# Large products of a two-layer hybrid trunk: one unsplit float32 matmul per weight tile instead of three on two-part operands

## The chip, the core and the metric

The kernel runs on one core of one Trainium2 chip. The metric is the device time of one execution in microseconds. The engines are named as the profile names them: PE (TensorE matmul), PEld (TensorE weight load), DVE (VectorE), ACT (ScalarE), POOL (GpSimd) and SP (SyncE, which here issues most transfers).

## The reference

Two layers run over 640 tokens of width 1024: 128 tokens of a prompt and 512 of a sample. Everything is float32.

```
for l in range(2):
    m  = silu(cond) @ w_mod + b_mod                       # nine vectors of 1024
    x  = rmsnorm(h) * (1 + sc1) + sh1
    h += 0.5 * g1 * (silu(x @ wg) * (x @ wu)) @ wd         # 1024 -> 2816 -> 1024
    x  = rmsnorm(h) * (1 + sc2) + sh2
    p  = x @ w_in                                         # 1024 -> 1536
    merged = [ssm(p), window_attention(p), full_attention(p), fourier(p)]
    h += g2 * merged @ w_out                              # 1024 -> 1024
    x  = rmsnorm(h) * (1 + sc3) + sh3
    h += 0.5 * g3 * (silu(x @ wg2) * (x @ wu2)) @ wd2
y = rmsnorm(h)
```

The four heads' inner products (attention, state space, Fourier) are small beside the products with `wg`, `wu`, `wd`, `w_in` and `w_out`; only these last five, called the large products here, are changed.

## The kernel before

The residual lies transposed in on-chip memory, channels on the partitions, in two halves of the tokens (`HALVES`): 256 and 384 columns. A large product takes a weight tile of 128x128 as the stationary operand and a block of 256 or 384 token columns as the moving one, and accumulates in PSUM over the blocks of 128 input channels (8 for 1024 channels). The projection `w_in` has it the other way for two of its three parts: 128 tokens are stationary, and 512 (or 256) weight columns move (`proj_tile`).

No large product is taken in float32 directly. Each operand is split into a high part, rounded to the type float32r, and a low part, the rest, also float32r. `mm3` (lines 258 to 265) then issues three matmuls for each weight tile: high by high, high by low, low by high. `ffn` has the same three written out for its first two feature blocks (lines 666 to 668), where four accumulations go on side by side because the inputs come ready block by block (`LEAD` = 2), and `proj_tile` has them at lines 1013 to 1015.

The split costs work on the other engines:

- Weights: `prep_to` (line 193) copies a piece of a loaded slab to `whi` on ACT (line 209) and subtracts on DVE to get `wlo` (line 210), in a ring of six pairs of buffers. Slabs of 1 MB at most come from HBM through SP into three buffers (`raw`), ahead by what `limit` and `load_limit` allow.
- Inputs: `x_prep` (line 539) makes `xh` on ACT and `xl` on DVE or POOL.
- The feature activations: after silu(gate) times up on DVE (`hx`, line 679) come `hh` on ACT (line 680) and `hl` on DVE (line 681).
- The merged heads: `split` makes a high part on ACT and a low one on DVE.

The order of instructions is that in which the Python code emits them, as the tile framework's scheduler then places them. Side work is emitted by `tick`: every large product reports how many nanoseconds its matmuls should take, and the norms, the stream of `w_mod` (on DVE, from POOL's queue) and the tables of the state space part are emitted when their due time in these nanoseconds has run out. `mm3` reports three times 0.417 ns a column plus 2.5 ns. Due times are `T_SUM` (2300, sum of squares), `T_BC` (5000, broadcast of the norm and `x_prep`), `T_OUT` (6500, output), and the spans `M_P0`, `M_P1` and `M_P2` over which `w_mod` is spread. At the end of each residual phase (`res_phase`) the last `FIN` output blocks run for one half of the tokens, then for the other, so that the first half's norm is made beside the second half's matmuls.

Other matmuls of the kernel are plain float32 already. Those of the Fourier part (`fnet`) are spoken of later. Each of its steps holds these calls, with float32 tiles on both sides, first those of the upper loop, at the end those of the lower one (shortened):

```python
for cs in range(2):
    for cb in range(2):
        nc.tensor.matmul(ps[:, 0:66], u[:, 0, c], dc[:, cs, :], start=True, stop=True)          # L1265
        for kb in range(4):
            nc.tensor.matmul(ps[:, 66:FC], u[:, 1 + kb, c], dl[:, cs, kb, :], ...)              # L1267
        yield
for nb in range(2):
    for half, (c0, w) in enumerate(HALVES):
        for mb in range(2):
            nc.tensor.matmul(ps[:, 0:w], fw[:, mb, ...], f[:, mb, c0:c0 + w], ...)              # L1293
```

Of the kernel before, what the change touches and what calls it, by code (L numbers as in the profile page):

```python
# [17 lines left out]
P = 128  # L18
# [19 lines left out]
FIN = 5  # L38
MARK = (-1, -1)
MARK_P = 5  # L40
# [4 lines left out]
M_P1 = 300  # L45
M_P2 = 340
X_PAT = ("dbdbdbdb", "dbbdbbdb")
# [61 lines left out]

class Net:  # L110
    def __init__(self, tc, a, depth=DEPTH, dump=None):
# [9 lines left out]
        self.ready = {}  # L121
        self.i_use = 0
        self.i_prep = 0
# [7 lines left out]
        self.limit = 0  # L131
        self.load_limit = 0
        self.seg = []
# [9 lines left out]
        self.ahead = 2  # L143
        self.fine = False
        self.marks = ()
# [29 lines left out]
    def load_upto(self, n):  # L175
        while self.i_load < min(n, len(self.slabs), self.load_limit):
            s = self.i_load
            srcs, shape = self.slabs[s]
            t = self.rawp.tile([P, RAW], F32, tag="raw", name="raw")
# [12 lines left out]

    def prep_to(self, n):
        while self.i_prep < min(n, len(self.wq), self.limit):
            sid, f = self.wq[self.i_prep]
            self.load_upto(sid + 1)
            v = f(self.raw[sid])
            k, w = v.shape[1], v.shape[2]
            sl = self.i_ring % self.ring_n
            self.i_ring += 1  # L200
            pool = self.ring_a if sl < RING_A else self.ring_b
            hi = pool.tile([P, 1024], F32R, tag=f"h{sl}", name="whi")
            lo = pool.tile([P, 1024], F32R, tag=f"l{sl}", name="wlo")
            hv = hi[:, 0:k * w].rearrange("p (k n) -> p k n", k=k)
            lv = lo[:, 0:k * w].rearrange("p (k n) -> p k n", k=k)
            with ExitStack() as es:
                for i in self.marks:
                    es.enter_context(self.tc.issue_after(i.ins))
                self.nc.scalar.activation(hv, v, AF.Copy)  # L209
                self.nc.vector.tensor_tensor(lv, v, hv, op=OP.subtract)  # L210
            self.ready[self.i_prep] = (hv, lv)
            self.slab_left[sid] -= 1
            if self.slab_left[sid] == 0:
                self.raw.pop(sid)
            self.load_upto(sid + self.raw_bufs)
            self.i_prep += 1

    def w(self, ahead=2):
        """Next operand of the stream; keeps `ahead` more in preparation."""
        i = self.i_use  # L220
        self.i_use += 1
        self.prep_to(i + 1 + ahead)
        return self.ready.pop(i)

# [43 lines left out]
    def setup(self):  # L268
# [5 lines left out]
        self.raw_bufs = 3  # L274
# [30 lines left out]
    def setup_vectors(self):  # L305
        """small vectors: rows of 128, transposed to columns."""
# [121 lines left out]
    def mod_to(self, n, ns=None):  # L428
        """slabs up to n: spread over the coming ns, or what is left of them now."""
# [46 lines left out]
    def load_x(self):  # L476
# [3 lines left out]
        xin = [self.xp.tile([P, w // P, D], F32, name=f"xin{i}", tag=f"xh{i}") for i, (_, w) in enumerate(HALVES)]  # L480
        junk = self.xp.tile([P, 2, D], F32, name="sqj", tag="xl0")
# [21 lines left out]
    def rstd_from(self, ss, c0, n):  # L503
        """ss [P, n] sums of squares per token -> rs_tok columns."""
# [6 lines left out]
    def norm_bc(self, half):  # L511
        """broadcast of rstd over the partitions, in PSUM [P, width]."""
# [13 lines left out]
    def x_tiles(self, half):  # L526
        w = HALVES[half][1]
        return (self.xp.tile([P, DB, w], F32R, name=f"xh{half}", tag=f"xh{half}"),
                self.xp.tile([P, DB, w], F32R, name=f"xl{half}", tag=f"xl{half}"))

    def x_norm(self, half, rb, k, x):
        """h * rstd of one block."""
        self.nc.vector.tensor_tensor(x, self.hT[half][:, k, :], rb[:, 0:HALVES[half][1]], op=OP.mult)

    def x_prep(self, half, l, j, rb=None, xn=None):
        """x = h rstd A + B as two parts; xn: h rstd, where it is there already."""
        nc = self.nc
        w = HALVES[half][1]
        self.x[half] = xh, xl = self.x_tiles(half)
# [3 lines left out]
        for k in range(DB):  # L543
            kind = X_PAT[half][k]
            t = self.t(w, "xt")
            for s, e, v in parts:
                Ak, Bk = A[:, k, v:v + 1], B[:, k, v:v + 1]
                if rb is None:
                    i_v = nc.vector.tensor_scalar(t[:, s:e], xn[:, k, s:e], Ak, Bk, op0=OP.mult, op1=OP.add)
                else:  # L550
                    i_v = nc.vector.scalar_tensor_tensor(t[:, s:e], self.hT[half][:, k, s:e], Ak, rb[:, s:e],  # L551
                                                         op0=OP.mult, op1=OP.mult)
                    if kind == "d":
                        i_a = nc.scalar.activation(xh[:, k, s:e], t[:, s:e], AF.Identity, bias=Bk)
                        nc.vector.scalar_tensor_tensor(xl[:, k, s:e], t[:, s:e], Bk, xh[:, k, s:e],
                                                       op0=OP.add, op1=OP.subtract)
                    else:
                        nc.scalar.activation(t[:, s:e], t[:, s:e], AF.Identity, bias=Bk)
            if rb is None or kind != "d":
                i_a = nc.scalar.activation(xh[:, k, :], t[:, 0:w], AF.Copy)  # L560
                nc.gpsimd.tensor_tensor(xl[:, k, :], t[:, 0:w], xh[:, k, :], op=OP.subtract)
            if k == (MARK[half] if rb is not None else MARK_P if half == 0 else -1):
                self.marks = (i_v, i_a)
# [33 lines left out]
    def finish_half(self, half, l, j):  # L597
        """norm of a finished half of the residual, spread over the coming matmuls."""
# [33 lines left out]
    def ffn(self, l, j, nxt, chunks, e_pro=None):  # L632
        """j: 0 or 2; nxt: (layer, norm) the next phase reads, or None.
        e_pro: the pool of the tables that are made beside the first N_TAB chunks."""
# [3 lines left out]
        for ci, (c0, n) in enumerate(chunks):  # L638
# [6 lines left out]
            hh = [hp.tile([P, nf, w], F32R, name=f"hh{i}", tag=f"hh{i}") for i, (_, w) in enumerate(HALVES)]  # L645
            hl = [hp.tile([P, nf, w], F32R, name=f"hl{i}", tag=f"hl{i}") for i, (_, w) in enumerate(HALVES)]

            def gate_up(fs, half, wts):
                w = HALVES[half][1]
                xh, xl = self.x[half]  # L650
# [10 lines left out]
                if len(fs) > 1:  # L661
                    for k in range(DB):
                        for i, f in enumerate(fs):
                            for s in range(2):
                                o, (wh, wl) = outs[2 * i + s], wts[f][s]
                                nc.tensor.matmul(o, wh[:, k, :], xh[:, k, :], start=(k == 0), stop=False)  # L666
                                nc.tensor.matmul(o, wl[:, k, :], xh[:, k, :], start=False, stop=False)
                                nc.tensor.matmul(o, wh[:, k, :], xl[:, k, :], start=False, stop=(k == DB - 1))  # L668
                        self.tick(len(fs) * 6 * (w * 0.417 + 2.5))
                else:  # L670
                    for s in range(2):
                        wh, wl = wts[fs[0]][s]
                        self.mm3(outs[s], [(wh[:, k, :], wl[:, k, :], xh[:, k, :], xl[:, k, :]) for k in range(DB)])
                for i, f in enumerate(fs):
# [10 lines left out]
            while f < n:  # L685
                grp = [f + i for i in range(lead if f == 0 else 1)]
                wts = {}
                for ff in grp:
                    wts[ff] = [self.w(self.ahead if len(grp) == 1 else 0) for _ in range(2)]
# [1135 lines left out]
```

## Time and profile before

| | |
|---|---|
| median of 3 runs | 2588.22 us (2588.08 to 2589.85) |
| span of the profiled execution | 2589.3 us |
| PE busy | 2517.7 us, 97% |
| DVE busy | 1507.6 us, 58% |
| ACT busy | 823.6 us, 32% |
| bytes read from HBM | 256.29 MB |

The profile is of one execution. A busy time is the union of an engine's instructions; matmuls overlap one another, so the mean duration of one is longer than the step from one to the next. The time that a matmul holds the engine is therefore read from the starts of neighbours in the timeline. A line number is that of the kernel before; L261 to L263 are the three matmuls of `mm3`, so that every large product through `mm3` shows under these lines.

### The profile page before, as it was taken

To read this page: it belongs to the slowest core of one execution; us is meant where nothing else is said; L and a number is where in the kernel's file an instruction comes from. 1 tells how busy PE (TensorE), PEld (TensorE's weight loads), DVE (VectorE), ACT (ScalarE), POOL (GpSimd) and SP (SyncE) were. 2 spreads that over 40 slices of the span, in tenths; PEclk is the share of its full clock that TensorE was granted. 3 is DMA by queue.
4 is the path that set the end of the run, shared out by engine and by line. 5 is a ranking of instruction groups with operands and counts; after the bars stand their busy time and mean duration, and the time that the engine had idled before them with its cause. 6 is when DMAs were issued, how large, how long until landed. Compare 5 with 4: busy or idle time off the path is not lost.

```text
span 2589.3 us, 41527 instructions
## 1 busy us (share of the span) xinstructions
PE 2517.7 (97%) x17054; PEld 2366.8 (91%) x17054; DVE 1507.6 (58%) x3012; ACT 823.6 (32%) x1547; POOL 387.2 (15%) x782
## 2 busy tenths in 40 slices
PE   5999999999899999999999999999999999999998
PEld 3899999998669899999999999999976799999998
DVE  6888677363667876454456666644546773333333
ACT  3332222242443532222233222223425553222222
POOL 2321111014801211000011001000183010000000
PEclk7999999999999999999999999999999999999999
DMA  7565444231114254333314445432401133222311
GB/s 254 158 182 183 145 147 147 90 101 55 34 35 147 58 168 126 119 111 114 114 50 143 137 125 151 139 106 66 126 18 54 34 98 98 69 82 62 98 49 41
DMA packets 199092, 273.93 MB, mean 106 GB/s; under 512 B 17208, under 2 KB 168472, under 8 KB 198392
## 3 DMA queue, kind: packets, MB, share of 16 engines
q1 hardware_dynamic: 176888, 193.30, 23.7%
q0 software_dynamic: 22016, 78.00, 10.2%
q8 instruction: 134, 2.20, 0.4%
q14 instruction: 54, 0.44, 0.1%
HBM read 256.29 MB, written 14.97 MB: 105 GB/s over the span
## 4 chain that ended last, share of the span: by engine, by line
PE 77%; issue 9%; POOL 7%; DVE 5%; DMA 2%; ACT 1%; SPq 0%; DVEq 0%; POOLq 0%; ACTq 0%
PE gu L261 14%; PE gu L263 14%; PE gu L262 14%; PE y L261 8%; PE y L262 8%; PE y L263 8%; POOL sc L1124 2%; POOL ee L1127 2%; POOL ee L1126 1%; DMA wm<-in_w_mod_dram 1%; POOL sc L1125 1%; DVE wlo L210 1%; DVE xt L551 1%; PE gu L668 1%; PE gu L666 1%
## 5 line engine op out<-in xcount | busy, mean ns | idle before, releaser
L261 PE MATMUL gu<-xh,whi 128*128 128x256 f32 (+1 forms) x2560 | 794.2, 310 | 0.9 <-DVE hx L679 0.9
L263 PE MATMUL gu<-xh,wlo 128*128 128x384 f32 (+1 forms) x2560 | 789.4, 309 | 0.6 <-DVE wlo L210 0.6
L262 PE MATMUL gu<-xl,whi 128*128 128x384 f32 (+1 forms) x2560 | 788.7, 308 | 0.0
L209 ACT ACTIVATE whi<-raw 128x1024 fp32r<-128x1024 f32 (+2 forms) x344 | 328.5, 960 | 875.4 <-PE gu L262 424.8
L210 DVE TENSOR_TENSOR wlo<-raw,whi 128x1024 fp32r<-128x1024 f32 (+2 forms) x344 | 380.2, 1107 | 343.3 <-ACT whi L209 342.9
L261 PEld LDWEIGHTS gu<-xh,whi 128*128 128x128 f32 x2560 | 481.3, 188 | 13.5 <-issue 11.0
L262 PEld LDWEIGHTS gu<-xl,whi 128*128 128x128 f32 x2560 | 482.6, 189 | 1.3 <-issue 1.2
L263 PEld LDWEIGHTS gu<-xh,wlo 128*128 128x128 f32 x2560 | 481.5, 188 | 1.6 <-DVE wlo L210 0.8
L261 PE MATMUL y<-hh,whi 128*128 128x384 f32 (+1 forms) x1408 | 436.0, 311 | 0.5 <-ACT est L957 0.3
L263 PE MATMUL y<-hh,wlo 128*128 128x384 f32 (+1 forms) x1408 | 434.8, 309 | 0.0
L262 PE MATMUL y<-hl,whi 128*128 128x384 f32 (+1 forms) x1408 | 434.6, 309 | 0.0
L389 DVE SCALAR_TENSOR_TENSOR mvec<-wm,cs,mvec 128x512 f32<-128x512 f32 x448 | 319.2, 750 | 20.9 <-DMA wm<-in_w_mod_dram 20.5
L595 DVE SCALAR_TENSOR_TENSOR hT<-y,G,hT 128x128 f32<-128x128 f32 (+1 forms) x432 | 175.8, 436 | 228.5 <-PE y L263 228.2
L261 PEld LDWEIGHTS y<-hh,whi 128*128 128x128 f32 x1408 | 266.1, 190 | 4.7 <-issue 3.7
L262 PEld LDWEIGHTS y<-hl,whi 128*128 128x128 f32 x1408 | 267.1, 190 | 0.5 <-issue 0.4
L263 PEld LDWEIGHTS y<-hh,wlo 128*128 128x128 f32 x1408 | 266.9, 190 | 0.0
L353 POOL DMA_DIRECT2D wm<-in_w_mod_dram x128 | 92.5, 723 | 956.7 <-DVE mvec L389 813.2
L679 DVE TENSOR_TENSOR hx<-sg,gu 128x256 f32<-128x256 f32 (+1 forms) x176 | 85.1, 483 | 119.5 <-ACT sg L677 119.2
L680 ACT ACTIVATE hh<-hx 128x256 fp32r<-128x256 f32 (+1 forms) x176 | 82.9, 471 | 184.6 <-DVE hx L679 184.5
L508 POOL TENSOR_TENSOR rst<-ms,mhalf 128x2 f32<-128x2 f32 (+1 forms) x12 | 11.2, 932 | 854.9 <-DVE ms L507 854.9
L677 ACT ACTIVATE sg<-gu 128x256 f32<-128x256 f32 (+1 forms) x176 | 75.3, 428 | 175.4 <-PE gu L263 170.8
L681 DVE TENSOR_TENSOR hl<-hx,hh 128x256 fp32r<-128x256 f32 (+1 forms) x176 | 86.3, 492 | 51.7 <-ACT hh L680 51.4
(313 smaller groups left out, 3239.8 us busy)
## 6 DMA issues: line engine op xcount, KB each, us to landing
wm<-in_w_mod_dram POOLq DMA_DIRECT2D x128, 512.0 KB, 4.2
raw<-in_ffn_w_gate_dram SPq DMA_DIRECT2D x44, 1024.0 KB, 5.4
raw<-in_ffn_w_up_dram SPq DMA_DIRECT2D x44, 1024.0 KB, 5.5
raw<-in_ffn_w_down_dram SPq DMA_DIRECT2D x24, 1024.0 KB, 5.2
raw<-in_ffn_w_down_dram SPq DMA_DIRECT2D x16, 768.0 KB, 4.9
raw<-in_w_in_dram SPq DMA_DIRECT2D x12, 1024.0 KB, 5.1
wm<-in_w_mod_dram SPq DMA_DIRECT2D x16, 512.0 KB, 5.5
raw<-in_ffn_w_down_dram SPq DMA_DIRECT2D x16, 512.0 KB, 4.1
```

What stands on the lines that cost most here:

```text
L209: self.nc.scalar.activation(hv, v, AF.Copy)
L210: self.nc.vector.tensor_tensor(lv, v, hv, op=OP.subtract)
L261: self.nc.tensor.matmul(out, wh, xh, start=(i == 0), stop=False)
L262: self.nc.tensor.matmul(out, wh, xl, start=False, stop=False)
L263: self.nc.tensor.matmul(out, wl, xh, start=False, stop=(i == n - 1))
L353: self.nc.gpsimd.dma_start(out=t.rearrange("p (j c) -> p j c", j=2), in_=w[kk * 256:(kk + 1) * 256, c0:c0 + 512].rearrange("(j p) c -> p j ...
L389: nc.vector.scalar_tensor_tensor(self.mvec[:, v], w, c, self.mvec[:, v], op0=OP.mult, op1=OP.add)
L595: nc.vector.scalar_tensor_tensor(h, y[:, s:e], G[:, k, v:v + 1], h, op0=OP.mult, op1=OP.add)
L677: nc.scalar.activation(sg[:, 0:w], g, AF.Silu)
L679: nc.vector.tensor_tensor(hx[:, 0:w], sg[:, 0:w], u, op=OP.mult)
L680: nc.scalar.activation(hh[half][:, f, :], hx[:, 0:w], AF.Copy)
L681: nc.vector.tensor_tensor(hl[half][:, f, :], hx[:, 0:w], hh[half][:, f, :], op=OP.subtract)
```

## The change

Every large product is one matmul on float32 operands. `mm3` becomes `mm`, the three matmuls in `ffn` and `proj_tile` become one, and `w()` hands out a view of the loaded slab. `prep_to`, the ring of split weights and the limits go; slabs come into four buffers of their own (`RAW_W`), and a slab is released by `used()` after the products that read it. `x_prep`, the activations and the merged heads write one float32 tile. The times reported to `tick` are those of `mm_ns`, and the spans of `w_mod`, `FIN` and the first chunks of the feature dimension (`CHUNKS4`) get other numbers.

```diff
-RING = 6
-RING_A = 2
+RAW_W = 4
-CHUNKS4 = ((0, 4), (4, 4), (8, 6), (14, 8))
+CHUNKS4 = CHUNKS
-FIN = 5
+FIN = 4
-M_P1 = 300
-M_P2 = 340
+M_P1 = 190
+M_P2 = 215
+def mm_ns(cols):
+    return cols * 0.835 + 3
...
-    def prep_to(self, n):
-        while self.i_prep < min(n, len(self.wq), self.limit):
...
-                self.nc.scalar.activation(hv, v, AF.Copy)
-                self.nc.vector.tensor_tensor(lv, v, hv, op=OP.subtract)
...
+    def w(self):
+        sid, f = self.wq[self.i_use]
+        self.i_use += 1
+        self.load_upto(sid + 1)
+        self.pend.append(sid)
+        return f(self.raw[sid])
+    def used(self):
+        for sid in self.pend:
             self.slab_left[sid] -= 1
             if self.slab_left[sid] == 0:
                 self.raw.pop(sid)
+        self.pend = []
+        self.load_upto((min(self.raw) if self.raw else self.i_load) + RAW_W)
...
-    def mm3(self, out, pairs):
+    def mm(self, out, pairs):
         n = len(pairs)
-        for i, (wh, wl, xh, xl) in enumerate(pairs):
-            self.nc.tensor.matmul(out, wh, xh, start=(i == 0), stop=False)
-            self.nc.tensor.matmul(out, wh, xl, start=False, stop=False)
-            self.nc.tensor.matmul(out, wl, xh, start=False, stop=(i == n - 1))
+        for i, (w, x) in enumerate(pairs):
+            self.nc.tensor.matmul(out, w, x, start=(i == 0), stop=(i == n - 1))
             if self.fine or i == n - 1:
-                self.tick((1 if self.fine else n) * 3 * (out.shape[-1] * 0.417 + 2.5))
+                self.tick((1 if self.fine else n) * mm_ns(out.shape[-1]))
...
+                    nc.vector.scalar_tensor_tensor(t[:, s:e], self.hT[half][:, k, s:e], Ak, rb[:, s:e],
+                                                   op0=OP.mult, op1=OP.mult)
+                    nc.scalar.activation(x[:, k, s:e], t[:, s:e], AF.Identity, bias=Bk)
...
-                    hx = self.t(w, "hx")
-                    nc.vector.tensor_tensor(hx[:, 0:w], sg[:, 0:w], u, op=OP.mult)
-                    nc.scalar.activation(hh[half][:, f, :], hx[:, 0:w], AF.Copy)
-                    nc.vector.tensor_tensor(hl[half][:, f, :], hx[:, 0:w], hh[half][:, f, :], op=OP.subtract)
+                    nc.vector.tensor_tensor(hx[half][:, f, :], sg[:, 0:w], u, op=OP.mult)
...
         for k in range(DB):
-            nc.tensor.matmul(ps[:, 0:n], h, wh, start=(k == 0), stop=False)
-            nc.tensor.matmul(ps[:, 0:n], h, wl, start=False, stop=False)
-            nc.tensor.matmul(ps[:, 0:n], lo, wh, start=False, stop=(k == DB - 1))
+            nc.tensor.matmul(ps[:, 0:n], x[:, k, c0:c0 + P], ws[k // kper][:, k % kper, :], start=(k == 0),
+                             stop=(k == DB - 1))
             if k % 4 == 3:
-                self.tick(12 * (n * 0.417 + 2.5))
+                self.tick(4 * mm_ns(n))
```

## Rows read from the trace of the kernel before

**Rows 1.** The page: span, and busy time, share and records of each engine

```profile
span 2589.3 us, 41527 instructions
PE 2517.7 (97%) x17054; PEld 2366.8 (91%) x17054; DVE 1507.6 (58%) x3012; ACT 823.6 (32%) x1547; POOL 387.2 (15%) x782
```

**Rows 2.** The page: the chain that ended last, by engine

```profile
PE 77%; issue 9%; POOL 7%; DVE 5%; DMA 2%; ACT 1%; SPq 0%; DVEq 0%; POOLq 0%; ACTq 0%
```

**Rows 3.** Stretches: length, busy us (records) of five engines, PE clock, DMA

```profile
54.00:100.00 46.00, 39.97 (x238) 36.63 (x239) 41.38 (x60) 17.93 (x35) 22.48 (x23) 0.88 0.32 102
558.00:852.00 294.00, 279.95 (x1753) 229.79 (x1752) 185.96 (x442) 118.47 (x269) 99.03 (x271) 0.97 0.25 76
852.00:900.00 48.00, 43.92 (x284) 41.04 (x283) 41.77 (x145) 23.45 (x52) 12.46 (x11) 0.93 0.09 21
1819.00:2109.00 290.00, 279.07 (x1779) 230.26 (x1778) 177.88 (x426) 121.15 (x273) 92.67 (x265) 0.98 0.22 68
```

**Rows 4.** Groups by line and shape: records | busy us, mean ns | idle before

```profile
L261 PE MATMUL gu<-xh,whi 128*128 128x256 f32 x1280 | 360.1, 281 | 0.0
L261 PE MATMUL y<-hh,whi 128*128 128x256 f32 x704 | 200.4, 285 | 0.3 <-ACT est L957 0.3
L261 PE MATMUL y<-xh,whi 128*128 128x256 f32 x128 | 36.2, 283 | 0.0
L666 PE MATMUL gu<-xh,whi 128*128 128x256 f32 x128 | 36.0, 292 | 2.3 <-ACT xh L560 2.3
L261 PE MATMUL pu<-xh,whi 128*128 128x256 f32 x32 | 9.1, 284 | 0.0
L1013 PE MATMUL pj<-whi,xh 128*128 128x512 f32 x160 | 63.8, 399 | 0.0
L1013 PE MATMUL pj<-whi,xh 128*128 128x256 f32 x80 | 23.0, 287 | 0.0
L1267 PE MATMUL f<-dl,P 128*128 128x258 f32 x64 | 15.7, 388 | 0.0
```

**Rows 5.** Timeline, PE, split products: start us, us, record

```profile
299.82 0.28 PE L261 MATMUL gu<-xh,whi 128*128 128x256 f32 x1
...
301.11 0.28 PE L263 MATMUL gu<-xh,wlo 128*128 128x256 f32 x1
...
306.90 0.34 PE L261 MATMUL gu<-xh,whi 128*128 128x384 f32 x1
...
310.37 0.34 PE L263 MATMUL gu<-xh,wlo 128*128 128x384 f32 x1
```

**Rows 6.** Timeline, PE, float32 matmuls of the Fourier part (x8: eight records merged)

```profile
650.55 0.33 PE L1265 MATMUL f<-fs,P 128*128 128x66 f32 x2
650.72 1.96 PE L1267 MATMUL f<-dl,P 128*128 128x258 f32 x8
652.52 0.60 PE L1373 MATMUL qkT<-ident,qr 128*128 128x128 f32 x4
...
1936.59 4.58 PE L1293 MATMUL f<-ff,fs 128*128 128x256 f32 x16 [0.69 <-ACT qs L1375]
...
1937.78 0.38 PE L1293 MATMUL f<-ff,fs 128*128 128x256 f32 x1
...
1938.85 0.38 PE L1293 MATMUL f<-ff,fs 128*128 128x256 f32 x1
1939.07 0.49 PE L1293 MATMUL f<-ff,fs 128*128 128x384 f32 x1
...
1940.68 0.49 PE L1293 MATMUL f<-ff,fs 128*128 128x384 f32 x1
```

**Rows 7.** The page: the low part of the weights' split on DVE

```profile
L210 DVE TENSOR_TENSOR wlo<-raw,whi 128x1024 fp32r<-128x1024 f32 (+2 forms) x344 | 380.2, 1107 | 343.3 <-ACT whi L209 342.9
```

**Rows 8.** Timeline around 850 us: broadcast of a norm, first input block after it

```profile
848.20 0.70 PE L521 MATMUL rb<-diag,ones 128*128 128x256 f32 x2 [0.91 <-DVE diag L518]
...
850.11 0.69 ACT L554 ACTIVATE xh<-xt,modT 128x128 fp32r<-128x128 f32 x2 [0.72 <-DVE xt L551]
```

More of the change, by code (lines that the diff above doesn't have):

```diff
@@ L175, in load_upto @@
     def load_upto(self, n):
-        while self.i_load < min(n, len(self.slabs), self.load_limit):
+        while self.i_load < min(n, len(self.slabs)):
             s = self.i_load
             srcs, shape = self.slabs[s]
-            t = self.rawp.tile([P, RAW], F32, tag="raw", name="raw")
+            t = self.wp.tile([P, 2048], F32, tag="raw", name="raw")
             n_el = 1
@@ L214, in prep_to @@
                 self.raw.pop(sid)
[L215 to L223, printed above, removed]
+        self.pend = []
+        self.load_upto((min(self.raw) if self.raw else self.i_load) + RAW_W)
     def later(self, ns, f):
@@ L479, in load_x @@
         ss = self.per.tile([P, 5], F32, name="ss_in", tag="ss", bufs=2)
-        xin = [self.xp.tile([P, w // P, D], F32, name=f"xin{i}", tag=f"xh{i}") for i, (_, w) in enumerate(HALVES)]
-        junk = self.xp.tile([P, 2, D], F32, name="sqj", tag="xl0")
+        xin = [self.xp.tile([P, w // P, D], F32, name=f"xin{i}", tag=f"x{i}") for i, (_, w) in enumerate(HALVES)]
+        junk = self.rawp.tile([P, RAW], F32, name="sqj", tag="raw")[:, 0:2 * D].rearrange("p (a b) -> p a b", a=2)
         xt = [xin[0][:, i] for i in range(2)] + [xin[1][:, i] for i in range(3)]
@@ L524, in norm_bc, with x_tile @@
         return rs
[L526 to L529, printed above, removed]
+    def x_tile(self, half):
+        return self.xp.tile([P, DB, HALVES[half][1]], F32, name=f"x{half}", tag=f"x{half}")
     def x_norm(self, half, rb, k, x):
@@ L538, in x_prep @@
         w = HALVES[half][1]
-        self.x[half] = xh, xl = self.x_tiles(half)
+        self.x[half] = x = self.x_tile(half) if xn is None else xn
         A = self.A[l, j]
@@ L543, in x_prep @@
         for k in range(DB):
-            kind = X_PAT[half][k]
-            t = self.t(w, "xt")
+            t = None if rb is None else self.t(w, "xt")
             for s, e, v in parts:
@@ L548, in x_prep @@
                 if rb is None:
-                    i_v = nc.vector.tensor_scalar(t[:, s:e], xn[:, k, s:e], Ak, Bk, op0=OP.mult, op1=OP.add)
+                    nc.vector.tensor_scalar(x[:, k, s:e], xn[:, k, s:e], Ak, Bk, op0=OP.mult, op1=OP.add)
                 else:
[L551 to L563, printed above, removed]
+                    nc.vector.scalar_tensor_tensor(t[:, s:e], self.hT[half][:, k, s:e], Ak, rb[:, s:e],
+                                                   op0=OP.mult, op1=OP.mult)
+                    nc.scalar.activation(x[:, k, s:e], t[:, s:e], AF.Identity, bias=Bk)
     def sq_start(self):
@@ L644, in ffn @@
                 nf = max(n for _, n in chunks[N_TAB:])
-            hh = [hp.tile([P, nf, w], F32R, name=f"hh{i}", tag=f"hh{i}") for i, (_, w) in enumerate(HALVES)]
-            hl = [hp.tile([P, nf, w], F32R, name=f"hl{i}", tag=f"hl{i}") for i, (_, w) in enumerate(HALVES)]
+            hx = [hp.tile([P, nf, w], F32, name=f"hx{i}", tag=f"hx{i}") for i, (_, w) in enumerate(HALVES)]
             def gate_up(fs, half, wts):
                 w = HALVES[half][1]
-                xh, xl = self.x[half]
+                x = self.x[half]
                 outs = []
@@ L664, in gate_up @@
                             for s in range(2):
[L665 to L669, printed above, removed]
+                                nc.tensor.matmul(outs[2 * i + s], wts[f][s][:, k, :], x[:, k, :], start=(k == 0),
+                                                 stop=(k == DB - 1))
+                        self.tick(len(fs) * 2 * mm_ns(w))
                 else:
                     for s in range(2):
-                        wh, wl = wts[fs[0]][s]
-                        self.mm3(outs[s], [(wh[:, k, :], wl[:, k, :], xh[:, k, :], xl[:, k, :]) for k in range(DB)])
+                        wt = wts[fs[0]][s]
+                        self.mm(outs[s], [(wt[:, k, :], x[:, k, :]) for k in range(DB)])
                 for i, f in enumerate(fs):
@@ L688, in ffn @@
                 for ff in grp:
-                    wts[ff] = [self.w(self.ahead if len(grp) == 1 else 0) for _ in range(2)]
+                    wts[ff] = [self.w() for _ in range(2)]
                 for half in range(2):
                     gate_up(grp, half, wts)
-                    if half == 0 and len(grp) > 1:
-                        self.prep_to(self.i_use + self.ahead)
+                self.used()
                 f += len(grp)
             last = ci == len(chunks) - 1
-            self.res_phase(n, [(hh[i], hl[i]) for i in range(2)], [(f, f) for f in range(n)], (l, j), nxt if last else None)
+            self.res_phase(hx, [(f, f) for f in range(n)], (l, j), nxt if last else None)
         hps.close()
@@ L1023, in proj_u @@
         uT = self.pp.tile([P, 2, 8, NCK], F32, name="uT", tag="ee")
-        wu = [self.w(0) for _ in range(2)]
-        self.prep_to(self.i_use + 2)
-        wf = None
+        wu = [self.w() for _ in range(2)]
+        wf = [self.w()]
         for half, (c0, w) in enumerate(HALVES):
@@ L1029, in proj_u @@
                 self.flush()
-            xh, xl = self.x[half]
+            x = self.x[half]
             for m in range(2):
                 ps = self.b([P, 512], name="pu")
-                self.mm3(ps[:, 0:w], [(wu[m][0][:, k, :], wu[m][1][:, k, :], xh[:, k, :], xl[:, k, :])
-                                      for k in range(DB)])
+                self.mm(ps[:, 0:w], [(wu[m][:, k, :], x[:, k, :]) for k in range(DB)])
                 self.evac(uT[:, m, :, c0 // 8:(c0 + w) // 8].rearrange("p j k -> p k j"),
                           ps[:, 0:w].rearrange("p (k j) -> p k j", j=8))
-            if wf is None:
-                wf = [self.w(0) for _ in range(2)]
-                self.prep_to(self.i_use + 2)
             if half == 1:
@@ L1222, in merged_tiles @@
     def merged_tiles(self):
-        self.mg = [self.x_tiles(h) for h in range(2)]
+        self.mg = [self.x_tile(h) for h in range(2)]
     def split(self, src, blk, c0, w, bias=None):
@@ L1231, in split @@
                 continue
[L1232 to L1233 removed]
+            o = self.mg[half][:, blk, s - h0:e - h0]
             v = src[:, s - c0:e - c0]
             if bias is None:
[L1236 to L1240 removed]
+                nc.scalar.activation(o, v, AF.Copy)
+            else:
+                nc.scalar.activation(o, v, AF.Identity, bias=bias)
     def fnet_load(self, l):
@@ L1544, in out1, with res_phase @@
                 y = self.b([P, 512], name="y1")
-                xh, xl = self.mg[half]
-                self.mm3(y[:, 0:w], [(wd[0][:, i, :], wd[1][:, i, :], xh[:, f, :], xl[:, f, :])
-                                     for i, f in enumerate(OUT1)])
+                x = self.mg[half]
+                self.mm(y[:, 0:w], [(wd[:, i, :], x[:, f, :]) for i, f in enumerate(OUT1)])
                 self.residual(half, db, y, self.G[l, 1])
+                if half == 1:
+                    self.used()
                 yield
-    def res_phase(self, n, xs, order, G, nxt, lead=1):
+    def res_phase(self, xs, order, G, nxt, lead=1):
         def one(db, half, wd):
@@ L1555, in one @@
             y = self.b([P, 512], name="y")
-            xh, xl = xs[half]
-            self.mm3(y[:, 0:w], [(wd[0][:, f, :], wd[1][:, f, :], xh[:, g, :], xl[:, g, :]) for f, g in order])
+            self.mm(y[:, 0:w], [(wd[:, f, :], xs[half][:, g, :]) for f, g in order])
             self.residual(half, db, y, self.G[G])
@@ L1567, in res_phase @@
             k = lead if db == 0 else 1
-            wds = [self.w(self.ahead) for _ in range(k)]
+            wds = [self.w() for _ in range(k)]
             for half in range(2):
@@ L1571, in res_phase @@
                     one(db + i, half, wds[i])
+            self.used()
             db += k
@@ L1574, in res_phase @@
             return
-        wds = [self.w(0) for _ in range(FIN)]
+        wds = [self.w() for _ in range(FIN)]
         h0, h1 = (1, 0) if nxt[1] is None else (0, 1)
@@ L1578, in res_phase @@
             one(DB - FIN + db, h0, wds[db])
-            self.prep_to(self.i_use + min(db, RING - FIN))
         self.x = [None, None]
@@ L1585, in res_phase @@
         self.fine = False
+        self.used()
         self.finish_half(h1, nxt[0], nxt[1])
@@ L1607, in mixer @@
         cva, cka = self.cache_v("cache_axial_kv", l, "cv1"), self.cache_k("cache_axial_kv", l, "ck1")
-        ws = [self.w(0) for _ in range(4)]
+        ws = [self.w() for _ in range(2)]
         for ti in range(5):
             self.proj(1, ti, ws)
-            self.prep_to(self.i_use + min(ti, 2))
             if ti == 0:
@@ L1621, in mixer @@
         self.qr = [qrt[:, 0], qrt[:, 1]]
-        ws = [self.w(0) for _ in range(4)]
+        ws = [self.w() for _ in range(2)]
         self.Pt.append(pp.tile([P, 5, 512], F32, name="P2", tag="P2"))
@@ L1741, in build @@
             n.proj_specs(l)
-            n.seg.append((len(n.wq), len(n.slabs)))
             n.out_specs(l)
             n.ffn_specs(l, "ffn2", CHUNKS4 if l + 1 < depth else CHUNKS)
-        n.seg.append((1 << 30, 1 << 30))
-        n.limit, n.load_limit = n.seg[0]
-        n.open_ring_a()
         e_pro, pro = n.open_pool("pro", side="right")
@@ L1751, in build @@
         n.load_x()
-        e_xs, xs = n.open_pool("xs", side="right")
-        xn = [xs.tile([P, DB, w], F32, name=f"xn{h}") for h, (_, w) in enumerate(HALVES)]
-        n.load_limit = 2
-        n.prep_to(2)
+        xn = [n.x_tile(h) for h in range(2)]
+        n.load_upto(2)
         for i in range(16):
@@ L1765, in build @@
         n.flush()
-        n.load_limit = n.seg[0][1]
+        n.load_upto(RAW_W)
         for h in range(2):
             n.x_prep(h, 0, 0, None, xn[h])
-        e_xs.close()
         n.job_ns = JOB_D
         n.e_mod.close()
-        n.open_ring_b()
         for l in range(depth):
@@ L1793, in build @@
         n.flush()
-        n.close_ring()
     n.es.close()
```

67 lines of the change are left out of this document (12 added, 55 removed).

## The prediction

> **What bounds the kernel now.** I read the busy shares first, then the chain, then the stretches in which PE is not full, and last the single steps of PE. PE is busy for 2517.7 of 2589.3 us, so 71.6 us are idle; no other engine but the weight loads beside it reaches 60% [rows 1]. The chain of work that ended last gives PE 77%, and POOL, the largest other engine, 7% [rows 2]. So the time is close to the sum of what PE is given. Its idle time lies in few places: 6.0 us in the start (54 to 100), 14.1 and 10.9 us in the two mixers, 4.1 us after the first mixer, and in these stretches the granted clock falls to between 0.88 and 0.98 of full speed [rows 3]. The other 36.5 us of idle time I leave as they are. What the reader is to see: a change in DVE or ACT work is worth little here, and a change in what one product costs on PE is worth nearly all of it.
>
> **How many products there are.** A row of one of the three lines counts the triples. Over 256 columns: 1280 + 128 (gate and up), 704 (down), 128 (output projection) and 32 (first projection) make 2272 triples [rows 4]; each weight tile also meets the other half of the tokens, so there are 2272 over 384 columns too. The rest of the projection has 160 triples over 512 and 80 over 256 columns [rows 4].
>
> **What a triple costs.** A matmul's mean duration, 281 ns over 256 columns [rows 4], is no price, since records overlap; the step from start to start is. From 299.82 to 301.11 us lie eleven steps over 256 columns: 117.3 ns each. From 306.90 to 310.37 us lie twenty over 384: 173.5 ns [rows 5]. That is 0.458 and 0.452 ns a column; for 512 columns I take 0.455, so 233 ns. A triple takes 352, 520.5 and 699 ns.
>
> **What one float32 call costs.** This is the term that decides. The kernel already has float32 calls with 128 rows and 128 columns of weights, fresh weights for each, in the Fourier part. In one step of its first loop the code makes one call at L1265 and four at L1267. The timeline has two records at L1265 and eight at L1267, and the next instruction starts 1.80 us after the first of the eight [rows 6]. Over the run L1267 has 64 records where the loops (2 by 2 by 4, two layers) make 32 calls; the split line L1013, which the loops call 160 times over 512 columns, has 160 [rows 4]. So a float32 call leaves two records and a float32r call one. The two do not run side by side: at L1293 eight calls leave 16 records, and six over 256 columns start from 1937.78 to 1938.85, 214 ns a step, six over 384 from 1939.07 to 1940.68, 322 ns a step [rows 6]. That is 0.836 and 0.839 ns a column for a record; I take 0.84, and 1.68 for a call: 430, 645 and 860 ns over 256, 384 and 512 columns. A far upper end is the 1.80 us for eight records of 258 columns, 0.872 ns a column, which has the switch from the product before in it. The step has the loading of the next weights beside it in these rows as it would have in the large products, so nothing is added for that.
>
> **A rule of the Trainium skill.** The page "FP8 and Floating Point Precision", section "TensorE Precision Notes", says that true FP32 takes four passes through the array. At one column per clock at 2.4 GHz that gives an estimate of 427 ns over 256 columns; by it the sum below would be some 20 us smaller, and the reading of one record as the whole call (215 ns) would be wrong. By that rule the trace agrees, with 430 ns for the two records of a call.
>
> **The change part by part.**
>
> Products. A pair (256 and 384 columns) goes from 352 + 520.5 = 872.5 to 430 + 645 = 1075 ns, 202.5 more; by 2272 that is 460.1 us. The 512-column products go from 699 to 860, 161 more by 160: 25.8 us. The 80 over 256 columns: 78 ns by 80, 6.2 us. Together **+492 us**, all on the path, since PE is full where they lie except for the gaps above.
>
> The split of weights leaves DVE by 380.2 us [rows 7] and ACT by a like number of copies; the low parts of inputs, activations and merged heads go too. I cost this at nothing: PE's work lies over it. What it can give is a part of the gaps: at the start the input blocks share DVE with it (DVE busy for 41.4 of 46 us), after the first mixer too (41.8 of 48) [rows 3]. At most all of 6.0 + 4.1 + 14.1 + 10.9 = 35.1 us comes back. I take 12, most of it from the start and the stretch after the first mixer, because the mixers' gaps come from the chain of the Fourier part and the scan on POOL, which are not touched.
>
> Loads. The bytes stay; a pair of 1 MB slabs (gate, up) now serves 32 pairs of products, 34 us of PE, against 28 before, with two more slabs behind it. Nothing waits for that. Releasing a slab waits for PE where it waited for the split; behind it on SP are later slabs and table transfers, which have the same longer time.
>
> Due times. The new reported time is 0.835 ns a column, half of the 1.68 that I expect, so side work comes at about half the pace in real time. The spans of `w_mod` (40 and 190 us, then 215) become about twice that, 460 and 430 us; a feed-forward phase has 528 pairs, 528 x 1.075 = 568 us, so they still end inside it. `T_BC` hurts in one place. At the end of a mixer's residual phase the second half has 4 x 4 products over 384 columns, 16 x 0.645 = 10.3 us; reported are 16 x 323.6 ns = 5178, so the 5000 of `T_BC` run out only with the last of them. The norm's broadcast then starts when PE has nothing left. From it to the end of the first input block the trace has 848.20 to 850.11 plus a half of 0.69, 2.3 us [rows 8]. Twice, at the two mixers' ends: 4.6 us, taken as 5. After a feed-forward phase the second half has twice as many products, 20.6 us, and the broadcast has ten of them left. Bounds: nothing, if the framework moves it forward; 2 x 5 us, if the clock falls in the gap.
>
> Fewer output blocks at the end (`FIN`) and the longer first chunks move no work on PE: nothing, unless the table work beside them comes due late, and its phase of 14 feature blocks has room (14 x 24 x 1.075 = 361 us).
>
> Sum: 2589.3 + 492 - 12 + 5 = 3074, against the profiled execution's own 2589.3; the median of the runs is 1.1 us below that, so no correction. I say **3075 us**, 19% more.
>
> **The rivals.** *One record is the call (faster).* If the second record of a float32 call were only another view of the same matmul, running beside the first, a call would cost 215, 323 and 430 ns, as `mm_ns` has it. A pair would go from 872.5 to 538: -334.5 by 2272 = -760 us, -269 x 160 = -43, -137 x 80 = -11, together -814: 1775 us, and some 1800 to 1840 with the scan and the stream of `w_mod` showing. For it: the program's own figure. Against it: the starts, in which the next call waits for both [rows 6]. It decides as soon as two calls follow each other at one record's step, and no row has that. 3%.
>
> *Waits come up (slower still).* PE does nothing else while it waits for an input, and all due times halve their pace. If each accumulation (some 600 of up to 8 and more calls) paid the switch that the 1.80 us show over eight plain steps of 217 ns, 0.064 us, that is 38 us; with late norms 10 us more: about 3120. 11%.
>
> *The gaps come back.* If the split on DVE and ACT was behind most of the gaps, all 35 us return and no new one comes: 2589.3 + 492 - 35 = 3046. 9%.
>
> **How the numbers follow.** My forecast, PE at two records a call with small change in the gaps, has 77%, 3060 to 3095 us with the rate's spread (0.836 to 0.842 ns a column is about 10 us on 2600). The range takes in both neighbours: **3042 to 3118 us**. Faster by over 0.2% is the first rival: 0.03. Within 0.2%, which is about what a measurement of this kernel can tell from no change: 0.01. Slower: 0.96.
>
> **What would show each step.** In the changed profile the lines of `mm` must show 2 records a call, and starts 215 and 322 ns apart; PE's records in the large products should go from three to two for each tile; PE should be busy for over 97% of the span at a clock near 1.0, DVE for about 1000 us and ACT for half of before. At the mixers' ends a wait of 2 to 5 us of PE for the norm's broadcast should stand. The prediction is wrong at its root if a call's two records overlap, and off in size if the large products' step is not 0.84 ns a column, or if a wait for slabs or for the inputs shows among PE's waits.

## The result and the profile after

The changed kernel takes 3061.8 us (median) against 2588.15 us; the ratio on record is 1.1822 (95% interval 1.1802 to 1.1842), that of the two medians 1.1830. A fourth execution took 6357.1 us, at a granted clock of 1.0, and is left out of the ratio; the other three lie between 3060.2 and 3062.0. The profiled execution has a span of 3060.2 us, 470.9 more than before, and the same mean granted clock, 0.985.

The first part of the page after, with busy time, share and records of each engine, then the chain by engine:

```profile
span 3060.2 us, 30185 instructions
PE 3008.0 (98%) x12270; PEld 2077.6 (68%) x12270; DVE 1001.1 (33%) x2333; ACT 404.1 (13%) x966; POOL 305.9 (10%) x721
...
PE 92%; POOL 4%; DMA 1%; issue 1%; DVE 1%; ACT 0%; SPq 0%; POOLq 0%; ACTq 0%
```

PE has 4784 fewer records and is busy for 490 us more [rows 1]. DVE falls by 506 us and ACT by 420, and the time does not follow them: the chain, which gave PE 77% before [rows 2], gives it 92%. That is how a change reads that takes work off the covered engines and puts it on the bounding one.

The groups of the large products by shape (records | busy us, mean ns), which answer to [rows 4]:

```profile
L240 PE MATMUL gu<-x,raw 128*128 128x256 f32 x2560 | 569.8, 380 | 0.0
L240 PE MATMUL y<-hx,raw 128*128 128x256 f32 x1408 | 319.6, 380 | 0.0
...
L240 PE MATMUL y<-x,raw 128*128 128x384 f32 x256 | 87.7, 488 | 0.0
...
L628 PE MATMUL gu<-x,raw 128*128 128x256 f32 x256 | 60.1, 394 | 4.5 <-ACT x L527 3.3 <-DVE x L523 1.2
L955 PE MATMUL pj<-raw,x 128*128 128x512 f32 x320 | 138.9, 593 | 0.0
```

Each count is twice that of one split line: 2560 for 1280, 1408 for 704, 256 for 128, 320 for 160. A float32 call leaves two records here as in the Fourier part. That the second one is time and not a copy is seen in the timeline of PE after (start us, us):

```profile
299.83 0.49 PE L240 MATMUL gu<-x,raw 128*128 128x384 f32 x1
300.15 0.49 PE L240 MATMUL gu<-x,raw 128*128 128x384 f32 x1
...
305.63 0.49 PE L240 MATMUL gu<-x,raw 128*128 128x384 f32 x1
```

Between 299.83 and 305.63 us lie 18 steps of 322 ns, the change from one accumulation to the next among them, and the step from one record to the next, 299.83 to 300.15, is the same. So a call over 384 columns holds PE for 644 ns, where the three split matmuls held it for 520 [rows 5].

The phases, in us, from the first matmul of each phase's product to that of the next (worked out from the timelines; the start and the end are what lies around them):

```
                    start  ffn1 l0  mixer 0  ffn2 l0  ffn1 l1  mixer 1  ffn2 l1   end     span
before               54.2    501.2    297.5    489.6    476.4    290.2    470.1  10.1   2589.3
after                52.2    594.4    332.3    589.2    582.5    328.2    571.7   9.7   3060.2
difference           -2.0    +93.2    +34.8    +99.6   +106.1    +38.0   +101.6  -0.4   +470.9
from the price               +106.9    +32.2   +106.9   +106.9    +32.2   +106.9         +492.0
```

"From the price" is the prediction's sum, put on the phases: 528 pairs at 202.5 ns in a feed-forward phase; 80 pairs, 80 products over 512 and 40 over 256 columns in a mixer. The third feed-forward phase, which had the fewest gaps before, comes out within 0.8 us of it. The first falls short by 13.7 us, the others by 7.3 and 5.3; the mixers go over by 2.6 and 5.8.

What PE waited for after (us in total, times, longest us):

```profile
PE macc L353 <- DMA wm<-in_w_mod_dram: 10.8, 10, 6.3
PE f L1227 <- DVE ff L1219: 5.9, 1, 5.9
PE f L1210 <- DVE ab L159: 5.1, 1, 5.1
PE gu L628 <- ACT x L527: 3.3, 2, 1.6
...
PE rb L498 <- DVE diag L495: 2.4, 2, 1.4
```

No wait for a slab of the large products' weights is among them; the first line is `w_mod` in the start, and both waits for `rb` lie in the start too. The two waits of the first gate product for the first input block stand at the two mixers' ends, where PE had none before; they are those that the due time `T_BC` was to cause.

### The profile page after: what moved, and what is told of

Read it like the earlier page. It is cut to its first block, busy times and chain, and to the rows that moved or that the text cites. A ratio compares the mean times of both kernels' runs of the same rounds, so it can differ in the third digit from the quotient of the medians.

```text
span 3060.2 us, 30185 instructions
## 1 busy us (share of the span) xinstructions
PE 3008.0 (98%) x12270; PEld 2077.6 (68%) x12270; DVE 1001.1 (33%) x2333; ACT 404.1 (13%) x966; POOL 305.9 (10%) x721
## 4 chain that ended last, share of the span: by engine, by line
PE 92%; POOL 4%; DMA 1%; issue 1%; DVE 1%; ACT 0%; SPq 0%; POOLq 0%; ACTq 0%
PE gu L240 45%; PE y L240 29%; PE gu L628 5%; PE pj L955 2%; PE O L1433 1%; DMA wm<-in_w_mod_dram 1%; PE pu L240 1%; POOL ee L1064 1%; POOL sc L1061 1%; PE S L1392 1%; POOL ee L1063 1%; POOL sc L1062 1%; PE S L1421 1%; PE Sb L1384 1%; PE macc L385 1%
## 5 line engine op out<-in xcount | busy, mean ns | idle before, releaser
L240 PE MATMUL gu<-x,raw 128*128 128x384 f32 (+1 forms) x5120 | 1393.2, 433 | 0.0
L240 PEld LDWEIGHTS gu<-x,raw 128*128 128x128 f32 x5120 | 968.4, 190 | 406.8 <-issue 10.8
L240 PE MATMUL y<-hx,raw 128*128 128x256 f32 (+1 forms) x2816 | 766.2, 433 | 0.0
L240 PEld LDWEIGHTS y<-hx,raw 128*128 128x128 f32 x2816 | 532.9, 190 | 222.0 <-issue 3.7
L955 PE MATMUL pj<-raw,x 128*128 128x512 f32 (+1 forms) x480 | 175.2, 522 | 0.0
L628 PE MATMUL gu<-x,raw 128*128 128x256 f32 (+1 forms) x512 | 145.4, 444 | 4.5 <-ACT x L527 3.3
L955 PEld LDWEIGHTS pj<-raw,x 128*128 128x128 f32 x480 | 90.6, 190 | 79.0 <-issue 72.2
L240 PE MATMUL y<-x,raw 128*128 128x384 f32 (+1 forms) x512 | 140.6, 434 | 0.0
L628 PEld LDWEIGHTS gu<-x,raw 128*128 128x128 f32 x512 | 99.1, 195 | 46.3 <-ACT x L527 4.4
L240 PEld LDWEIGHTS y<-x,raw 128*128 128x128 f32 x512 | 96.2, 190 | 39.0 <-issue 0.7
L541 ACT ACTIVATE sqt<-hT 128x256 f32<-128x256 f32 (+1 forms) x84 | 39.4, 468 | 224.8 <-DVE hT L559 206.3
L542 DVE TENSOR_TENSOR sq<-sq,sqt 128x256 f32<-128x256 f32 (+1 forms) x84 | 41.3, 492 | 44.5 <-ACT sqt L541 44.5
L525 DVE SCALAR_TENSOR_TENSOR xt<-hT,A,rbs 128x128 f32<-128x128 f32 (+1 forms) x120 | 43.3, 435 | 16.2 <-ACT rbs L500 16.2
```

Of the source, the lines that this page charges most:

```text
L240: self.nc.tensor.matmul(out, w, x, start=(i == 0), stop=(i == n - 1))
L541: nc.scalar.activation(t[:, 0:w], self.hT[half][:, k, :], AF.Square)
L542: nc.vector.tensor_tensor(self.sqacc[half], self.sqacc[half], t[:, 0:w], op=OP.add)
L628: nc.tensor.matmul(outs[2 * i + s], wts[f][s][:, k, :], x[:, k, :], start=(k == 0), stop=(k == DB - 1))
L955: nc.tensor.matmul(ps[:, 0:n], x[:, k, c0:c0 + P], ws[k // kper][:, k % kper, :], start=(k == 0), stop=(k == DB - 1))
```

## The experiments

The theory: the time is what PE is given, and a float32 call costs two records of 0.84 ns a column. The rivals: the new buffers, releases and due times cost the time, or the split on DVE and ACT was itself a part of the bound.

**The products alone.** The kernel before gets one float32 matmul for three, and keeps its split, ring and due times.

```diff
-            hi = pool.tile([P, 1024], F32R, tag=f"h{sl}", name="whi")
+            hi = pool.tile([P, 1024], F32, tag=f"h{sl}", name="whi")
...
-            self.nc.tensor.matmul(out, wh, xh, start=(i == 0), stop=False)
-            self.nc.tensor.matmul(out, wh, xl, start=False, stop=False)
-            self.nc.tensor.matmul(out, wl, xh, start=False, stop=(i == n - 1))
+            self.nc.tensor.matmul(out, wh, xh, start=(i == 0), stop=(i == n - 1))
```

The same is done in `ffn` and `proj_tile`, and `xh` and `hh` become float32.

> The kernel before with one float32 matmul in place of each three, everything else as before: the high parts are float32 copies, and the low parts are still made on DVE and POOL but no matmul reads them. Theory (the float32 call's two records set the time, the split lies under PE): the products cost what they cost in the changed kernel, and only the gaps at the starts of the feed-forward phases, some 25 us, stay, so 3060 to 3090 us. Rival (the new buffers, releases and due times of the changed kernel cost the time): near 2590, in any case under 2750. Rival (the freed DVE and ACT matter more than thought): over 3110.

Measured: 3067.53 us, ratio 1.1849 (1.1823 to 1.1875), inside the theory's bounds. The page of this run, and its line of the weights' low part:

```profile
PE 3001.4 (98%) x12270; PEld 2071.8 (68%) x12270; DVE 1518.4 (50%) x3012; ACT 815.8 (27%) x1547; POOL 381.5 (12%) x782
...
L210 DVE TENSOR_TENSOR wlo<-raw,whi 128x1024 fp32r<-128x1024 f32 (+2 forms) x344 | 380.2, 1107 | 325.5 <-ACT whi L209 324.7
```

PE has the records of the changed kernel, DVE and ACT have the work of the kernel before, and the time is that of the changed kernel but for 5.7 us. So the products alone give the whole loss. What else differs, the split's work (380 us of `wlo` and more) on one side, the buffers, releases and due times on the other, comes to 5.7 us net beside products this slow; the two were not taken apart, and the intervals of the two ratios overlap. The phases are 600.5, 332.6, 590.2, 582.5, 325.9 and 573.2 us: against the changed kernel the first is 6.1 longer, and the others differ by 2.3 at most. PE is idle once in that phase, for a product of DVE, which is busy for 41.3 of the phase's first 48.2 us (24.4 of 48.0 in the changed kernel):

```profile
PE gu L664 <- DVE hx L675: 5.5, 1, 5.5
```

The phases that fall short of the price do so here too, by 7.6, 6.3 and 3.8 us. So most of what came back came back with the split's work still there: PE's slower products cover it.

**The split's low parts alone.** Three float32r matmuls a tile stay; the low parts are not made, and all three matmuls take the high parts, so the refinement is left out.

```diff
-                self.nc.vector.tensor_tensor(lv, v, hv, op=OP.subtract)
...
-            lv = lo[:, 0:k * w].rearrange("p (k n) -> p k n", k=k)
+            lv = hv
...
-                    nc.vector.tensor_tensor(hl[half][:, f, :], hx[:, 0:w], hh[half][:, f, :], op=OP.subtract)
```

> The kernel before with its three float32r matmuls a weight tile, but without the low parts: they are not made, and the second and third matmul repeat the first, so the result is not refined. PE gets the same work, DVE some 500 us less. Theory (PE bound, split covered): 2555 to 2589 us, the gaps at the starts of the phases coming back. Rival (the split was part of the bound): under 2540.

Measured: 2559.44 us, ratio 0.9882 (0.9861 to 0.9903): 28 us less than the kernel before in the same comparison (2587.5). Inside the theory's bounds, at their lower part. The stretch from 54 to 100 us of this run, which answers to the first of [rows 3]:

```profile
54.00:100.00 46.00, 44.31 (x303) 42.49 (x304) 33.56 (x73) 21.95 (x46) 8.53 (x13) 0.92 0.52 166
```

PE gets 303 records through where it got 238 [rows 3], and DVE is busy for 33.6 of 46 us instead of 41.4. So the low parts did hold PE up at the start: the first phase is 14.1 us shorter, the mixers 5.1 and 7.7. Taking the low parts away is worth 28 us beside the faster products; taking them and the copies away, with the new buffers and due times, came to 5.7 net beside the slower ones. A gap has no price of its own: it depends on how long the bounding engine takes beside it.

**Two records a tile.** As the last, with two of the three matmuls.

```diff
             self.nc.tensor.matmul(out, wh, xh, start=(i == 0), stop=False)
-            self.nc.tensor.matmul(out, wh, xl, start=False, stop=False)
             self.nc.tensor.matmul(out, wl, xh, start=False, stop=(i == n - 1))
```

> As the run without low parts, with two float32r matmuls a weight tile instead of three (both high by high): 235 and 347 ns a tile over 256 and 384 columns, close to the 215 and 323 that a float32 call of one record would have cost. 2272 x 0.2908 + 160 x 0.233 + 80 x 0.117 = 707 us less than the run without low parts. If PE still bounds all of it, about 1865 us; if the scan on POOL and the stream of w_mod show as the first rival of the prediction had it, 1890 to 1930; if another engine becomes the bound, over 1950.

Measured: 1944.77 us, ratio 0.7518 (0.7492 to 0.7543). It is 615 us less than with three records, not 707, and lies between the second and the third expectation. The page and the first waits of PE in this run:

```profile
PE 1838.6 (95%) x12270; PEld 1686.1 (87%) x12270; DVE 1008.5 (52%) x2381; ACT 809.3 (42%) x1547; POOL 312.1 (16%) x721
...
PE 69%; POOL 9%; DMA 7%; issue 6%; DVE 5%; ACT 3%; SPq 1%; DVEq 0%; POOLq 0%; ACTq 0%
...
PE pe L1083 <- issue: 15.1, 2, 7.7
...
PE rb L518 <- DVE diag L515: 8.9, 6, 1.9
PE py L1167 <- ACT Sx L1140: 7.3, 2, 4.5
```

By phases, 52 of the 92 us that are missing lie in the two mixers (272.7 and 261.2 us), and 20 in the first feed-forward phase. In the mixers PE is idle for 25.7 and 22.2 us, where the run with three records has 8.9 and 5.7, and the mean clock is 0.92 and 0.95 where that run has 0.96 and 0.99. PE waits there before the first product of the state space part (`pe`; the profile names no releaser) and for what follows the scan (`py`). The record count is that of the changed kernel, 12270, and the time is 1117 us less: what a record costs counts, and not how many there are.

**One record a tile.** The high parts alone: operands rounded to float32r, one matmul.

```diff
-            self.nc.tensor.matmul(out, wh, xh, start=(i == 0), stop=False)
-            self.nc.tensor.matmul(out, wh, xl, start=False, stop=False)
-            self.nc.tensor.matmul(out, wl, xh, start=False, stop=(i == n - 1))
+            self.nc.tensor.matmul(out, wh, xh, start=(i == 0), stop=(i == n - 1))
```

> As before with one float32r matmul a weight tile. Another 707 us would leave about 1160 us if PE bounded everything. Theory: by now transfers and the mixers' chains (scan on POOL, softmax) come up, so 1300 to 1600 us and PE busy for under 90%. If it still falls by 700 us, PE was the bound even there.

Measured: 1577.17 us, ratio 0.609 (0.606 to 0.612). This is inside the theory's bounds, with PE busy for 77%. Page, chain, and the first waits of PE:

```profile
PE 1216.2 (77%) x7486; PEld 1026.3 (65%) x7486; DVE 996.7 (63%) x2381; ACT 789.2 (50%) x1547; POOL 313.3 (20%) x721
...
PE 32%; DMA 20%; DVE 16%; issue 13%; POOL 11%; ACT 6%; SPq 1%; POOLq 0%; DVEq 0%; ACTq 0%
...
PE macc L404 <- DVE mvec L385: 88.5, 23, 8.7
PE gu L259 <- DVE hx L670: 28.9, 17, 8.1
PE pss L579 <- DVE sq L571: 28.8, 10, 9.3
```

The third step brings 368 us of 707. PE is no longer the bound: the chain gives it 32%, and by line the stream of `w_mod` is what comes next (its transfers 16%, DVE's accumulation 7%). Beside the kernel before it rounds all operands of the large products, so it is another kernel in what it computes.

**The same with `w_mod` spread wider.** The mechanism of that wait, tried on the last run.

```diff
-M_P1 = 300
-M_P2 = 340
+M_P1 = 380
+M_P2 = 420
```

> As the run with one float32r matmul a weight tile (operands rounded to float32r, no low parts), with w_mod spread over 380 and 420 reported microseconds instead of 300 and 340. There PE waited most for DVE's accumulation of w_mod (88.5 us on the sum over partitions). Theory (it is the pace of w_mod on DVE against a phase that is now three times shorter on PE): 1520 to 1565 us. Rival (the phase is bound by the total of w_mod whatever its pace): 1570 to 1590 us.

Measured: 1562.59 us, ratio 0.6034 (0.6019 to 0.6049), at the upper end of what was expected.

```profile
PE macc L404 <- DVE mvec L385: 67.0, 18, 8.6
PE pss L579 <- DVE sq L571: 39.4, 10, 9.3
PE gu L259 <- DVE hx L670: 25.3, 8, 8.5
```

The wait falls from 88.5 to 67.0 us, and the next one, for the sum of squares on the same DVE, rises from 28.8 to 39.4. So the pace matters a little. Whether the total of `w_mod` sets the rest was not tried. This is the fastest kernel of the study, with the rounding named above.

**The due times of the norm.** The changed kernel with

```diff
-T_SUM = 2300
-T_BC = 5000
+T_SUM = 1150
+T_BC = 2500
```

> The changed kernel with T_SUM 1150 and T_BC 2500, so that the sum of squares and the norm's broadcast are due at the same real time as before the change. Theory (at the two mixers' ends PE waits for the broadcast because the reported nanoseconds are half the real ones): the two waits of PE at the first input block, 1.65 us each, go, and some clock with them: 3055 to 3060 us. Rival (the waits come from the chain of the norm itself and not from its due time): the waits stay, 3060 to 3063 us.

Measured: 3064.95 us, ratio 1.1834 (1.1807 to 1.1861), not to be told from the changed kernel. PE's waits:

```profile
PE rb L498 <- DVE diag L495: 8.0, 5, 1.9
...
PE gu L628 <- ACT x L527: 0.6, 1, 0.6
```

The due time was the cause of the two waits for the input block, 3.3 us after the change and 0.6 now. But the broadcast's own matmul (`rb`) now stands in PE's queue ahead of the last output products before DVE has made its operand: that wait goes from 2.4 to 8.0 us. The 5.6 us that are new lie at the ends of three feed-forward phases (629.9, 1552.1 and 2136.7 us, 1.8 to 1.9 each), whose second half has twice the products: there the 5000 of the changed kernel cost no wait, and 2500 come too early. The mechanism holds, and the gain does not come: the theory's time was wrong.

**`w_mod` later in the kernel before.** A try to get the start's gap back without touching the split.

```diff
-M_P0 = 40
+M_P0 = 32
...
                     n.mod_to(24, M_P0 * 1e3)
+                    n.m_ns = 18e3
```

> The kernel before, split and all, with the stream of w_mod on DVE starting 18 reported microseconds into the first feed-forward phase instead of 5, at 4 us a slab instead of 5. In the first phase the run without low parts was 14 us faster than the kernel before, the largest part of its gain. Theory (there DVE has the input blocks, the low parts and w_mod at once, and PE waits for the sum of them): PE starts fuller and 4 to 9 us go, 2579 to 2585 us. Rival (the low parts alone hold PE up): 2586 to 2590 us.

Measured: ratio 1.0004 (0.9984 to 1.0024), no difference. DVE's timeline at the start of the phase shows why it tells nothing:

```profile
51.88 2.90 DVE L549 TENSOR_SCALAR xt<-xn,A,modT 128x128 f32<-128x128 f32 x5
54.70 0.87 DVE L387 TENSOR_SCALAR mvec<-wm,cs 128x512 f32<-128x512 f32 x2
...
61.45 1.75 DVE L210 TENSOR_TENSOR wlo<-raw,whi 128x1024 fp32r<-128x1024 f32 x1
```

`w_mod` (`mvec`) begins 3.6 us after the first matmul of the phase, which in this run started at 51.1 us, among the input blocks. In the kernel before, whose phase starts at 54.2, it begins 3.6 us in as well:

```profile
57.79 0.87 DVE L387 TENSOR_SCALAR mvec<-wm,cs 128x512 f32<-128x512 f32 x2
```

So the edit did not move it on DVE, and neither expectation was tested; why it did not move stays open. Which of the three works on DVE holds PE up at the start stays open between the low parts and their sum with `w_mod`; the run without low parts shows only that without them most of the gap goes.

## Why the prediction was right

The forecast was 3075 us, the time is 3061.8: 1.1822 measured against 1.19.

- *PE bounds, and other work is worth little.* Right. With DVE and ACT as before, the time is the changed kernel's within 5.7 us; in the kernel before, the low parts were worth 28 us, about 1%.
- *A float32 call leaves two records, 0.84 ns a column each.* Right: twice the counts, and 322 ns a step over 384 columns, the value read from eight calls of the Fourier part [rows 6]. This was the step on which the sign hung, since one record as the whole call gave 1775 us. What settled it was to count the calls in the loops against the records; a mean duration alone (388 ns over 258 columns [rows 4]) would have priced the call too low, and the program's own figure of 0.835 ns a column would have led to the other side. By the rule of the Trainium skill's "FP8 and Floating Point Precision", "TensorE Precision Notes" (four passes for true FP32), the trace after agrees: 644 ns over 384 columns, where four times 384 columns at one a clock of 2.4 GHz give an estimate of 640.
- *+492 us for the products.* Right to 1 us where the phase had no gaps before (106.1 for 106.9).
- *12 us of gaps come back.* The term that was mis-sized. The phases give 27.1 us back in the feed-forward parts and 2.4 around them, and the mixers take 8.4 more than their price. And the reason was in the main another: I put the return down to the split leaving DVE and ACT. With the split kept, 492 - 477 = 15 us come back all the same (its span is 3066.6), beside slower products; the removal, with the new buffers and due times, adds 6 net. Nor was PE's idle time the bound on what could return, as I took it: in the four feed-forward phases it falls by 13.1 us only (from 13.4 to 0.3), half of the 27.1. The rest was booked as busy. In the stretch from 54 to 100 us before, 124 records over 256 columns and 96 over 384 would take 31 us at the price, an estimate, and with 18 small ones the profile books 40.0; part of that is the clock, 0.88 there [rows 3].
- *5 us of new waits at the mixers' ends.* The place and the cause were right, the size 3.3 us. That the mixers grew by more is not from there. After the change PE is idle there for 12.2 and 10.5 us, less than the 14.1 and 10.9 of before, but at mean clocks of 0.95 and 0.96 where these were 0.97 and 0.98 [rows 3]. The rows of the mixers after (length, busy us of PE, PEld, DVE, ACT and POOL, then PE clock):

```profile
646.60:978.90 332.30, 320.06 (x1499) 213.27 (x1497) 156.44 (x383) 96.03 (x239) 87.45 (x266) 0.95 0.21 64
...
2150.60:2478.80 328.20, 317.71 (x1500) 210.42 (x1498) 145.39 (x362) 96.72 (x238) 80.74 (x259) 0.96 0.17 52
```

  A lower mean clock over 330 us would be of the right size, 3 us for a hundredth; that it is the cause was not tried. With the old due times and the split kept, the mixers go over their price by 2.9 and 3.5 us too, at 0.95 and 0.97.
- *The sum.* The products were forecast at +492, all else at -7; all else came to -21. These 14 us are most of what lies between 3075 and the measured time; the two mis-sized terms, the gaps and the mixers, erred in opposite directions.
- *The range.* Its upper end rested on a switch of 0.064 us in each accumulation. There is none in the large products: records over 384 columns follow each other at 322 ns across accumulations too.
- *The first rival.* Its time was at best at its lower limit. Two float32r records a tile, 235 and 347 ns, gave 1945 us; at the prices of that rival the pairs would take 100 us less and the projection 7, so no less than some 1838 us even if all of it came back, the top of the 1800 to 1840 that I gave. Of the 707 us that the next step took off PE only 368 came back, so the time would lie higher: what is not PE's work costs more when PE is fast than I allowed.

## What to carry to other kernels

Before pricing an operation from a profile, count its records against the calls in the code, and read its price from start to start. Three rounded matmuls at 0.455 ns a column each, 1.37 together, beat one float32 call at 1.68, although the splitting costs hundreds of microseconds on two other engines, because those engines lie under the bound. And the worth of that covered work is no constant: the low parts cost 28 us beside fast products, and beside slow ones the low parts and copies together, net of the new buffers and due times, 6. Nor is idle time a bound on that worth: half of what came back in the feed-forward phases had been booked as busy.

## What the runs showed of the hardware

- A float32 call is not four thirds of three float32r ones. A float32r record takes 0.452 to 0.458 ns a column, more than the 0.417 of one column a clock at 2.4 GHz, while half a float32 record takes 0.42. So the one call costs 22 to 24% more than the three, 430 to 352 and 645 to 520 ns, and not 33%.
- The loads of weights do not set the step in either. Each record has a load of its own, of 188 ns on the page before and 190 after, while the step over 256 columns of float32r is 117 ns and that of float32 215: by their records, loads lie beside the products, and beside one another.

```profile
L261 PEld LDWEIGHTS gu<-xh,whi 128*128 128x128 f32 x2560 | 481.3, 188 | 13.5 <-issue 11.0
L240 PEld LDWEIGHTS gu<-x,raw 128*128 128x128 f32 x5120 | 968.4, 190 | 406.8 <-issue 10.8
```
